# First layer's attention in a transformer kernel: heads handled in pairs that lie on different halves of the partitions, and six score buffers in place of three

## The chip, the core and the metric

The kernel runs on one core of a Trainium2 chip. A core has TensorE (matrix products, results in the eight banks of PSUM), VectorE, ScalarE, GpSimd and SyncE, which issues most transfers; they run side by side and wait for each other through semaphores. The metric is the device time of one execution in microseconds (us), as the median of several runs. Beside it stands one execution that was recorded by the profiler, with the start and duration of every instruction.

## What is computed

Two blocks on 256 tokens of 1024 features, in float32. The first block has an attention layer and a retention layer, each with a SwiGLU product and modulated by adaLN; the second block has two hybrid layers (convolution, latent attention, dilated attention). The change touches the attention of the first layer: 16 heads of 64 features, eight with stick-breaking and eight with a causal softmax (MoBA with one block of 256 keys, which is its own block, so that nothing else is selected).

```python
def stick_breaking_attention(q, k, v):
    ...
        z = jnp.einsum('bhqd,bhkd->bhqk', qb, k).astype(jnp.float32) * scale
        qpos = start + jnp.arange(SB_QBLOCK)
        strict = kpos[None, :] < qpos[:, None]
        log_1mb = jnp.where(strict, jax.nn.log_sigmoid(-z), 0.0)
        after = lax.cumsum(log_1mb, axis=3, reverse=True) - log_1mb
        a = jnp.where(strict, jnp.exp(jax.nn.log_sigmoid(z) + after), 0.0)
        return jnp.einsum('bhqk,bhkd->bhqd', a.astype(v.dtype), v)
...
def moba_attention(q, k, v):
    ...
        s_own = jnp.einsum('bhqd,bhkd->bhqk', qb, k_own).astype(jnp.float32) * scale
        kpos_own = own * MOBA_BLOCK + kpos_in
        s_own = jnp.where(kpos_own[None, :] <= qpos[:, None], s_own, NEG)
        p = jax.nn.softmax(jnp.concatenate([s_past, s_own], axis=-1), axis=-1).astype(v.dtype)
        ...
def attn_hybrid_mixer(h, w_qkv, w_o, pos):
    ...
    sb = stick_breaking_attention(q[:, :N_SB_HEADS], k[:, :N_SB_HEADS], v[:, :N_SB_HEADS])
    qm = rotary(q[:, N_SB_HEADS:], pos)
    km = rotary(k[:, N_SB_HEADS:], pos)
    mb = moba_attention(qm, km, v[:, N_SB_HEADS:])
    o = jnp.concatenate([sb, mb], axis=1).transpose(0, 2, 1, 3).reshape(B, S, ATT_W)
    return o @ w_o
```

## The kernel before

Every large product is done in three parts (mm3, L381): activations and weights are each split into a high and a low part in TensorE's faster float32 form, and hi*hi, hi*lo and lo*hi are summed. The split of the weights is made on the chip: SyncE loads a chunk of 128 x 2048 into one of a few `raw` buffers (L325), ScalarE casts it (whi, L345), VectorE subtracts (wlo, L346). In the same buffers come the weights of adaLN, which VectorE multiplies and sums as a side task (acc, L541); `rate` says how many such steps are added per weight chunk. Their results are split (L456, L457) and broadcast by TensorE with ones_r.

The order on TensorE is written out by hand: it runs its instructions in the order in which the program emits them. A planner keeps a clock `now` of planned TensorE work. A side task is a generator (Job) that yields for how long to leave it alone; `tick`, called behind each mm3, runs the tasks whose due time has come. The other engines' order is set by the compiler's scheduler, which prefers what was emitted earlier and takes what is ready by its own model.

In layer0 (L786) `startup` makes the modulation, the first norm, and q, k (ps0) and v of the stick-breaking heads. Then main products on w_qkv for q, k and v of the MoBA heads run (gemm_col), and the attention of the first eight heads is a side task among them; MoBA's attention is a side task among the product for v and the output product on w_ao (gemm_k). A head of 64 features lies on one half of the 128 partitions of qT and kT: even heads on partitions 0 to 63, odd heads on 64 to 127.

- sb_job (L621) takes one stick-breaking head: two score products into a bank of PSUM (of 256 and of 128 columns, each done as two passes in the trace), three ScalarE steps Abs, Exp, Ln into a tile sbe (three buffers, L629 to L631), two VectorE steps that form the masked sums in a tile named sbs (tag sm, three buffers, L632, L634); after D_SB = 9.42 us of planned work three products with a triangle (ntri) and with minus ones (sq in the trace) on top of the scores, then Exp on ScalarE (L639) and the mask on VectorE (L640) into aT.
- causal_job (L587) takes one MoBA head (and one MLA head in the second block): two score products, masked maximum on VectorE (L598), Exp with sum on ScalarE (L602), reciprocal (L604), normalisation (L606); after D_SOFT = 11.39 us of planned work three transposes (L281) and a copy into aT (L608). The tile sm has three buffers in layer 0.
- score (L830) is the task of one head; it waits till q and k are there. Heads are spawned with due times SP_SB = 2.55 and SP_MB = 2.65 us apart. av (L839) does the products with v of two heads when all eight heads are done; their results lie on different halves of the columns of the array.
- epi (L821) turns a block of q or k of the MoBA heads by the rotary factors on VectorE (L582 to L585, tiles rows and rt) out of the block's bank; D_ROT0 = 5.49 us later they are transposed and copied (L828) to qT, kT.

A bank of PSUM comes from one pool of eight (`bank`). It is free when its last reader is done.

## Time and profile before

| | |
|---|---|
| time, median of 3 runs | 1525.12 us (1524.68 to 1526.28) |
| profiled execution, its span | 1522.7 us |
| TensorE (PE) busy | 1487.4 us, 98% |
| weight loads (PEld) busy | 1237.7 us, 81% |
| VectorE (DVE) busy | 1026.6 us, 67% |
| ScalarE (ACT) busy | 800.0 us, 53% |
| GpSimd (POOL) busy | 93.0 us, 6% |
| DMA, mean | 201 GB/s |

TensorE's products overlap: a product starts before the one ahead of it has ended, so the distance between starts, not the duration, is what a product costs in a stream. Shares of the whole span hide that stages have different limits; the stage of the change lies between 69 and 167 us. PE, PEld, DVE, ACT, POOL and SP are the engines' names in the rows; a q behind a name is the engine's instruction queue. L277 is the line of every matrix product, L281 that of every transpose: they are told apart by the tiles.

### The profile page before, as it was taken

What the parts mean: (1) busy time and instruction counts of PE and PEld (TensorE: products, weight loads), DVE (VectorE), ACT (ScalarE), POOL (GpSimd) and SP (SyncE); (2) the same over time, 40 slices, a digit from 0 to 9 for tenths busy, and PEclk for the clock granted to TensorE, in tenths of its full rate; (3) what the DMA queues carried; (4) which work ended last, traced back from release to release, by engine and by line L of the source; (5) the groups of instructions that cost most, each with busy time, mean ns of one, the idle gap of its engine ahead of it and who ended that gap; (6) DMA issues with size and microseconds to landing.
All of it is one profiled execution on the core that took longest, in us unless ns stands there. A gap on an engine that the chain in (4) does not pass through costs nothing.

```text
span 1522.7 us, 19655 instructions
## 1 busy us (share of the span) xinstructions
PE 1487.4 (98%) x7508; PEld 1237.7 (81%) x7508; DVE 1026.6 (67%) x1605; ACT 800.0 (53%) x1297; POOL 93.0 (6%) x84
## 2 busy tenths in 40 slices
PE   7989999999999999999999999999999999999998
PEld 4776788887877888888787899988888779998887
DVE  4698888748988767655577565555666866555564
ACT  4657455534544544544457655565545765555551
POOL 0000000000010000000020011100001101111000
PEclk9999999999999999999999999999999999999999
DMA  9667587755776648654355354444545535444442
GB/s 381 258 227 273 204 293 296 276 187 193 294 256 241 228 144 301 236 195 173 109 185 182 124 196 157 163 169 170 180 159 184 179 129 192 159 159 176 176 172 81
DMA packets 52961, 306.62 MB, mean 201 GB/s; under 512 B 7546, under 2 KB 10490, under 8 KB 24580
## 3 DMA queue, kind: packets, MB, share of 16 engines
q1 hardware_dynamic: 52148, 305.14, 55.9%
q8 instruction: 59, 0.97, 0.3%
q10 hardware_dynamic: 720, 0.24, 0.1%
q14 instruction: 34, 0.28, 0.1%
HBM read 301.16 MB, written 1.05 MB: 198 GB/s over the span
## 4 chain that ended last, share of the span: by engine, by line
PE 85%; DVE 6%; DMA 3%; ACT 2%; POOL 1%; issue 1%; DVEq 0%; POOLq 0%; ACTq 0%
PE p L277 81%; PE p L281 5%; DMA raw<-in_w_in_dram 3%; DVE wlo L346 2%; ACT whi L345 1%; POOL qss L452 1%; POOL ss L485 1%; DVE junk L493 0%; DVE res L520 0%; DMA raw<-in_w_ao_dram 0%; DVE acc L541 0%; DMA x<-in_x_dram 0%; DVE x L521 0%; ACT sm L602 0%; ACT sbe L630 0%
## 5 line engine op out<-in xcount | busy, mean ns | idle before, releaser
L346 DVE TENSOR_TENSOR wlo<-raw,whi 128x1024 fp32r<-128x1024 f32 (+2 forms) x474 | 541.7, 1162 | 196.4 <-ACT whi L345 191.1
L345 ACT CAST whi<-raw 128x1024 fp32r<-128x1024 f32 (+2 forms) x474 | 467.9, 1002 | 290.2 <-PE p L277 209.9
L277 PE MATMUL p<-whi,hh 128*128 128x512 f32 (+1 forms) x1504 | 590.9, 393 | 6.8 <-ACT mqT L1223 3.8
L277 PE MATMUL p<-whi,hl 128*128 128x512 f32 (+1 forms) x1504 | 566.8, 377 | 3.2 <-DVE hl L457 2.7
L277 PE MATMUL p<-wlo,hh 128*128 128x512 f32 (+1 forms) x1504 | 565.5, 376 | 0.0
L277 PEld LDWEIGHTS p<-whi,hh 128*128 128x128 f32 x1504 | 283.3, 188 | 56.3 <-issue 6.7
L277 PEld LDWEIGHTS p<-whi,hl 128*128 128x128 f32 x1504 | 282.9, 188 | 49.9 <-DVE hl L457 3.9
L277 PEld LDWEIGHTS p<-wlo,hh 128*128 128x128 f32 x1504 | 283.9, 189 | 40.6 <-issue 1.7
L541 DVE SCALAR_TENSOR_TENSOR acc<-raw,csc,acc 128x1024 f32<-128x1024 f32 x80 | 102.4, 1280 | 4.9 <-DMA raw<-in_ada_w_dram 4.0
L277 PE MATMUL p<-whi,ah 128*128 128x512 f32 x176 | 70.0, 398 | 0.0
L277 PE MATMUL p<-whi,al 128*128 128x512 f32 x176 | 69.5, 395 | 0.0
L277 PE MATMUL p<-wlo,ah 128*128 128x512 f32 x176 | 69.5, 395 | 0.0
L452 POOL TENSOR_TENSOR dss<-dss,mh 128x6 f32<-128x6 f32 x32 | 42.3, 1322 | 345.7 <-DVE dss L451 328.7
L1337 DVE TENSOR_TENSOR rows<-p,dss 128x384 f32<-128x384 f32 x32 | 17.9, 558 | 45.6 <-POOL dss L452 45.6
L916 ACT ACTIVATE fth<-p 128x256 f32<-128x256 f32 x44 | 16.9, 383 | 58.1 <-PE p L277 58.0
L485 POOL TENSOR_TENSOR ss<-ss,mh 128x1 f32<-128x1 f32 x14 | 13.8, 988 | 489.9 <-DVE ss L484 489.9
L277 PE MATMUL p<-whi,s 128*128 128x512 f32 x128 | 41.3, 397 | 0.0
L277 PEld LDWEIGHTS p<-whi,al 128*128 128x128 f32 x176 | 33.0, 187 | 8.1
L277 PEld LDWEIGHTS p<-wlo,ah 128*128 128x128 f32 x176 | 33.0, 188 | 7.8
L277 PEld LDWEIGHTS p<-whi,ah 128*128 128x128 f32 x176 | 33.0, 188 | 7.8
L277 PEld LDWEIGHTS p<-dk,dq 64*128 64x128 f32 x256 | 30.8, 187 | 9.8 <-issue 8.0
L277 PE MATMUL p<-whi,yh 128*128 128x512 f32 x96 | 38.4, 400 | 0.0
(251 smaller groups left out, 1579.7 us busy)
## 6 DMA issues: line engine op xcount, KB each, us to landing
raw<-in_w_in_dram SPq DMA_DIRECT2D x48, 1024.0 KB, 4.8
raw<-in_w_gu_dram SPq DMA_DIRECT2D x44, 1024.0 KB, 5.9
raw<-in_ada_w_dram SPq DMA_DIRECT2D x40, 1024.0 KB, 6.8
raw<-in_w_in_dram SPq DMA_DIRECT2D x48, 768.0 KB, 4.5
raw<-in_w_ret_dram SPq DMA_DIRECT2D x24, 1024.0 KB, 5.0
raw<-in_w_dn_dram SPq DMA_DIRECT2D x22, 1024.0 KB, 4.9
raw<-in_w_qkv_dram SPq DMA_DIRECT2D x11, 1024.0 KB, 5.6
as<-in_ada_s_dram SPq DMA_DIRECT2D x16, 512.0 KB, 8.5
```

Source lines behind the costliest of these rows:

```text
L277: self.T.matmul(out, lhsT=lhsT, rhs=rhs, start=first, stop=last, skip_group_check=skip)
L281: self.T.transpose(out, in_, self.ident)
L345: for ins in (self.A.copy(hi[:, :m * n], src), self.V.tensor_tensor(lo[:, :m * n], src, hi[:, :m * n].bitcast(F32), ALU.subtract)):
L346: self.V.tensor_tensor(lo[:, :m * n], src, hi[:, :m * n].bitcast(F32), ALU.subtract)):
L452: self.G.tensor_tensor(ss, ss, self.mh[:, :n], ALU.pow)
L485: self.G.tensor_tensor(ss[:, 0:1], ss[:, 0:1], self.mh[:, 0:1], ALU.pow)
L541: self.V.scalar_tensor_tensor(acc, r[:, j * D:j * D + D], self.sc[:, k:k + 1], acc, ALU.mult, ALU.add)
L916: A.activation(th, ps[:, 0:256], AF.Silu)
L1337: V.tensor_tensor(rows[:, :384].rearrange("p (h d) -> p h d", d=64), ps.rearrange("p (h d) -> p h d", d=64), ss[:, :6, None].to_broadcast( ...
```

## The change

Heads of the first layer are taken in pairs. score now stands for a pair: both heads get their aT tile and their bank at once, and the score products alternate: the first product of the even head (partitions 0 to 63), the first of the odd head (64 to 127), then the second of each. All ScalarE and VectorE steps of the two heads follow, head by head. The second steps (products with ntri and nones, or transposes) come for the first head after the same planned delay, and for the second head D_SB2 = 1.8 (stick-breaking) or SP_MB = 2.65 us (MoBA) later. Stick-breaking pairs are spawned 6.2 us apart, MoBA pairs 2 x 2.65. The planned cost of a pair's score products is that of one head. The tag sm has six buffers in layer 0 in place of three, and the stick-breaking scratch e (three buffers of the same size) is gone: the head's own aT tile holds it. MLA calls the same new function with one head; its planned cost is 0.218 in place of 0.214 for the first product, everything else there is as before.

```diff
-SP_SB, SP_MB, SP_MLA, SP_DIL = 2.55, 2.65, 13.59, 4.5
+SP_SB, D_SB2, SP_MB, SP_MLA, SP_DIL = 6.2, 1.8, 2.65, 13.59, 4.5
...
-    def causal_job(self, q, k, scale, aT):
+    def causal_heads(self, heads, scale, gap):
         V, A = self.V, self.A
-        qT, kT = q(), k()
-        ps = self.bank()
-        self.mm(ps[:, 0:128], qT[:, 0:128], kT[:, 0:128])
-        self.mm(ps[:, 128:384], qT[:, 128:256], kT, us=0.432)
-        sm = self.ph.tile([128, 384], F32, tag="sm", bufs=self.smb, name=self.nm("sm"))
...
+        n = len(heads)
+        ps = [self.bank() for _ in heads]
+        for p, (qT, kT, _) in zip(ps, heads):
+            self.mm(p[:, 0:128], qT[:, 0:128], kT[:, 0:128], us=0.218 / n)
+        for p, (qT, kT, _) in zip(ps, heads):
+            self.mm(p[:, 128:384], qT[:, 128:256], kT, us=0.432 / n)
...
-        yield D_SOFT if self.smb != 2 else D_SOFTM
-        A.copy(aT, self.trs(sm, 3))
+        yield D_SOFT if n == 2 else D_SOFTM
+        for i, (sm, (_, _, aT)) in enumerate(zip(sms, heads)):
+            if i:
+                yield gap
+            A.copy(aT, self.trs(sm, 3))
...
-    def sb_job(self, q, k, aT):
+    def sb_heads(self, heads, gap):
+
         V, A = self.V, self.A
-        qT, kT = q(), k()
-        ps = self.bank()
-        self.mm(ps[:, 0:256], kT[:, 0:128], qT, True, True, 0.432, True)
-        self.mm(ps[:, 256:384], kT[:, 128:256], qT[:, 128:256], False, True, 0.216, True)
-        e = self.ph.tile([128, 384], F32, tag="sbe", bufs=3, name=self.nm("sbe"))
-        sp = self.ph.tile([128, 384], F32, tag="sm", bufs=self.smb, name=self.nm("sbs"))
...
+        ps = [self.bank() for _ in heads]
+        for p, (qT, kT, _) in zip(ps, heads):
+            self.mm(p[:, 0:256], kT[:, 0:128], qT, True, True, 0.216, True)
+        for p, (qT, kT, _) in zip(ps, heads):
+            self.mm(p[:, 256:384], kT[:, 128:256], qT[:, 128:256], False, True, 0.109, True)
...
+        for p, (_, _, aT) in zip(ps, heads):
+            e = aT.rearrange("p j n -> p (j n)")
+            sp = self.ph.tile([128, 384], F32, tag="sm", bufs=self.smb, name=self.nm("sbs"))
+            A.activation(e, p[:, :384], AF.Abs)
...
         yield D_SB
...
+        for i, (p, sp, (_, _, aT)) in enumerate(zip(ps, sps, heads)):
+            if i:
+                yield gap
+            self.mm(p[:, 0:256], self.ntri, sp[:, 0:256], False, True, 0.432, True)
...
-            self.ph, self.smb = p, 3
+            self.ph, self.smb = p, 6
...
-            for hd in range(8):
-                sj[hd] = self.spawn(score(hd, j0), 1.0 + hd * SP_SB)
             for pr in range(4):
...
+                sj[pr] = self.spawn(score(pr, j0), 1.0 + pr * SP_SB)
+            for pr in range(4):
...
-            for hd in range(8, 16):
-                sj[hd] = self.spawn(score(hd, qkj), 0.5 + (hd - 8) * SP_MB)
+            for pr in range(4, 8):
+                sj[pr] = self.spawn(score(pr, qkj), 0.5 + (pr - 4) * 2 * SP_MB)
```

## Rows read from the trace of the kernel before

**Rows 1.** Busy time by stretch: stretch, length, engines, clock, DMA share, GB/s

```profile
82.00:98.00 16.00, 12.62 (x70) 10.84 (x71) 15.56 (x27) 8.82 (x17) 0.00 (x0) 1.00 0.63 224
129.00:146.50 17.50, 15.46 (x72) 10.68 (x70) 16.77 (x42) 15.88 (x47) 0.00 (x0) 1.00 0.69 248
167.00:300.00 133.00, 133.00 (x607) 109.11 (x607) 109.10 (x126) 66.93 (x98) 4.33 (x4) 1.00 0.78 286
```

**Rows 2.** TensorE's timeline, stick-breaking: start us, us, instruction, count

```profile
71.45 2.06 PE L277 MATMUL p<-qT,kT 64*128 64x256 f32 x16 [0.35 <-ACT qT L815]
...
75.41 0.39 PE L277 MATMUL p<-whi,hl 128*128 128x512 f32 x1
...
76.91 0.39 PE L277 MATMUL p<-wlo,hh 128*128 128x512 f32 x1
...
88.13 1.04 PE L277 MATMUL p<-sbs,sq 128*128 128x256 f32 x6
88.92 0.47 PE L277 MATMUL p<-whi,hh 128*128 128x512 f32 x1
```

**Rows 3.** TensorE's timeline, MoBA's first scores

```profile
114.16 1.46 PE L277 MATMUL p<-kT,qT 64*128 64x256 f32 x10 [0.47 <-ACT kT L828]
115.55 0.50 PE L277 MATMUL p<-whi,hh 128*128 128x512 f32 x1
...
116.45 0.92 PE L277 MATMUL p<-kT,qT 64*128 64x128 f32 x4
```

**Rows 4.** TensorE's timeline, products with v and the output product's end

```profile
146.47 2.82 PE L277 MATMUL p<-aT,v 128*64 128x256 f32 x32
...
157.02 0.39 PE L277 MATMUL p<-acch,ones_r 128*128 128x512 f32 x1
...
157.95 0.39 PE L277 MATMUL p<-whi,oTq 128*128 128x512 f32 x1
...
163.56 1.03 PE L281 MATMUL p<-ident,junk 128*128 128x128 f32 x8
```

**Rows 5.** TensorE's timeline, its longest wait in the first layer

```profile
97.78 0.63 PE L281 MATMUL p<-ident,rows 128*128 128x128 f32 x4 [3.38 <-DVE rows L585]
```

**Rows 6.** Waits from 60 to 170 us: who for whom, us, times, longest

```profile
PE p L281 <- DVE rows L585: 3.7, 2, 3.4
...
PE p L277 <- ACT aT L608: 1.0, 2, 0.7
PE p L281 <- ACT sm L606: 0.9, 2, 0.7
...
PEld p L277 <- ACT qT L828: 0.6, 1, 0.6
ACT sm L606 <- DVE st L604: 0.5, 2, 0.3
```

**Rows 7.** VectorE's timeline in the first layer's attention

```profile
74.32 0.56 DVE L632 SCALAR_TENSOR_TENSOR sbs<-p,sbe 128x384 f32<-128x384 f32 x1 [1.22 <-ACT sbe L631]
...
87.71 0.56 DVE L632 SCALAR_TENSOR_TENSOR sbs<-p,sbe 128x384 f32<-128x384 f32 x1 [0.43 <-PE p L277]
...
94.22 1.28 DVE L541 SCALAR_TENSOR_TENSOR acc<-raw,csc,acc 128x1024 f32<-128x1024 f32 x1
95.41 0.42 DVE L584 TENSOR_TENSOR rt<-p,rope 128x256 f32<-128x256 f32 x1
...
103.16 1.23 DVE L346 TENSOR_TENSOR wlo<-raw,whi 128x1024 fp32r<-128x1024 f32 x1 [0.82 <-ACT whi L345]
...
119.44 0.28 DVE L598 CUSTOM_DVE_ANT_0 sm<-p,causal 128x128 f32<-128x128 f32 x1
...
129.02 0.29 DVE L598 CUSTOM_DVE_ANT_0 sm<-p,causal 128x128 f32<-128x128 f32 x1 [1.88 <-PE p L281]
```

**Rows 8.** ScalarE's timeline, the last copy of probabilities

```profile
144.47 0.48 ACT L608 COPY aT<-p 128x384 f32<-128x384 f32 x1
```

**Rows 9.** SyncE's timeline, the load of the last chunk of w_ao

```profile
131.52 0.34 SPq L325 DMA_DIRECT2D raw<-in_w_ao_dram  x1
```

More of the change, by code (lines that the diff above doesn't have):

```diff
@@ new lines, in causal_heads @@
+        n = len(heads)
[4 more added lines that the diff above has]
+            self.mm(p[:, 128:384], qT[:, 128:256], kT, us=0.432 / n)
+        halves = ((0, 128), (128, 384))
+        sms = []
+        for p in ps:
+            sm = self.ph.tile([128, 384], F32, tag="sm", bufs=self.smb, name=self.nm("sm"))
+            st = self.wk.tile([128, 6], F32, tag="st", bufs=8, name=self.nm("st"))
+            for t, (c0, c1) in enumerate(halves):
+                V.tensor_tensor_reduce(sm[:, c0:c1], p[:, c0:c1], self.causal[:, c0:c1], 1.0, NEG, ALU.add, ALU.max,
+                                       st[:, t:t + 1])
+            V.tensor_scalar_mul(st[:, 2:4], st[:, 0:2], -scale)
+            for t, (c0, c1) in enumerate(halves):
+                A.activation(sm[:, c0:c1], sm[:, c0:c1], AF.Exp, bias=st[:, 2 + t:3 + t], scale=scale,
+                             accum_out=st[:, 4 + t:5 + t])
+            V.reciprocal(st[:, 4:6], st[:, 4:6])
+            for t, (c0, c1) in enumerate(halves):
+                A.activation(sm[:, c0:c1], sm[:, c0:c1], AF.Copy, scale=st[:, 4 + t:5 + t])
+            sms.append(sm)
@@ new lines, in sb_heads @@
+        ps = [self.bank() for _ in heads]
[3 more added lines that the diff above has]
+            self.mm(p[:, 256:384], kT[:, 128:256], qT[:, 128:256], False, True, 0.109, True)
+        d2 = lambda x: x.rearrange("p (j n) -> p j n", n=128)[:, 0:3:2]
+        sps = []
+        for p, (_, _, aT) in zip(ps, heads):
+            e = aT.rearrange("p j n -> p (j n)")
+            sp = self.ph.tile([128, 384], F32, tag="sm", bufs=self.smb, name=self.nm("sbs"))
+            A.activation(e, p[:, :384], AF.Abs)
+            A.activation(e, e, AF.Exp, scale=-1.0)
+            A.activation(e, e, AF.Ln, bias=1.0)
+            V.scalar_tensor_tensor(sp, p[:, :384], 0.0, e, ALU.max, ALU.add)
+            V.tensor_tensor(d2(sp), d2(sp), self.strict, ALU.mult)
+            sps.append(sp)
@@ L828, in epi, with score @@
                 A.copy((qT if b == 1 else kT)[1][:, :, t * 128:t * 128 + 128], self.trs(rows, 4))
-            def score(hd, deps):
-                j, r = hd // 8, hd % 8
-                pr, o = r // 2, (r % 2) * 64
+            def score(pr, deps):
+                j, r = pr // 4, pr % 4
                 while not all(d.done for d in deps):
                     yield 0.7
-                aTs[hd] = aT = p.tile([128, 3, 128], F32, tag="aT", bufs=AT0, name=self.nm("aT"))
-                q, k = (lambda: qT[j][o:o + 64, pr]), (lambda: kT[j][o:o + 64, pr])
-                yield from self.sb_job(q, k, aT) if j == 0 else self.causal_job(q, k, 0.125, aT)
+                heads = []
+                for i in range(2):
+                    aTs[2 * pr + i] = aT = p.tile([128, 3, 128], F32, tag="aT", bufs=AT0, name=self.nm("aT"))
+                    heads.append((qT[j][64 * i:64 * i + 64, r], kT[j][64 * i:64 * i + 64, r], aT))
+                yield from self.sb_heads(heads, D_SB2) if j == 0 else self.causal_heads(heads, 0.125, SP_MB)
             def av(pr, deps):
@@ L849, in layer0 @@
             ch = chunks_of(D, QKV_BLOCKS)
-            for hd in range(8):
-                sj[hd] = self.spawn(score(hd, j0), 1.0 + hd * SP_SB)
             for pr in range(4):
-                avj[pr] = self.spawn(av(pr, [sj[i] for i in range(8)]), 1.0)
+                sj[pr] = self.spawn(score(pr, j0), 1.0 + pr * SP_SB)
+            for pr in range(4):
+                avj[pr] = self.spawn(av(pr, [sj[i] for i in range(4)]), 1.0)
             qkj = self.gemm_col(h, "w_qkv", ch[1:3], epi, 1)
-            for hd in range(8, 16):
-                sj[hd] = self.spawn(score(hd, qkj), 0.5 + (hd - 8) * SP_MB)
+            for pr in range(4, 8):
+                sj[pr] = self.spawn(score(pr, qkj), 0.5 + (pr - 4) * 2 * SP_MB)
             vj = self.gemm_col(h, "w_qkv", ch[3:4], epi, 3)
             for pr in range(4, 8):
-                avj[pr] = self.spawn(av(pr, vj + [sj[i] for i in range(8, 16)]), 1.0)
+                avj[pr] = self.spawn(av(pr, vj + [sj[i] for i in range(4, 8)]), 1.0)
             gate, = self.finish(jobs[0])
@@ L1292, in pair @@
                 aTs.append(p.tile([128, 3, 128], F32, tag="maT", bufs=4, name=self.nm("maT")))
-                yield from self.causal_job(lambda: qT[:, hd], lambda: kT[:, hd], 96.0 ** -0.5, aTs[j])
+                yield from self.causal_heads([(qT[:, hd], kT[:, hd], aTs[j])], 96.0 ** -0.5, 0.0)
             yield 1.5
```

25 lines of the change are left out of this document (4 added, 21 removed).

## Prediction, made before the changed kernel ran

> **What bounds the kernel now.** I read the page's first section for the balance of the engines, then the busy time by stretch, then TensorE's timeline through the stretch that the change touches, then the waits and the timelines of VectorE and ScalarE there. The table by stretch says where a saving counts [rows 1]. From 167 us TensorE is busy 133.00 of 133.00 us: what the first layer gains by then is kept, since nothing behind it waits for another engine for long. In the first layer's attention, 69 to 167 us, it is not so: VectorE is busy 15.56 of 16.00 us from 82 to 98, ScalarE 15.88 of 17.50 us from 129 to 146.5. The granted clock is 1.00 in these stretches, so durations of one may be used in another. Three engines take turns as the limit here, and the gain is what the other two leave of TensorE's saving.
>
> **What a head's score product costs on TensorE.** A head alone is four passes, two of 256 and two of 128 columns, on 64 partitions. The last main product (512 columns) before one starts at 75.41, the second one behind it at 76.91: 1.50 us [rows 2], in which two products at their usual distance of 0.23 (four from 157.02 to 157.95, [rows 4]) take 0.46. So a head alone costs 1.04 us. How much of that is streaming? Six passes of the second step (two of 256, four of 128 columns) take from 88.13 to 88.92 [rows 2], so some 0.2 and 0.1 us each, and four score passes some 0.6. The other 0.4 us surrounds them.
>
> Do two halves of the partitions run side by side? The kernel before shows it where heads happen to be neighbours: ten passes (six of 256, four of 128 columns) lie between 114.16 and 115.55, 1.39 us with the surroundings [rows 3], where one after the other they would stream 1.6 and need 2.0. And eight heads' products with v, which alternate between halves of the columns, take 2.82 us for 32 passes [rows 4] that would stream 4.8. I take full overlap: a pair costs what a head alone costs, 1.04. Bounds: 1.04 (full) and 1.6 (0.6 + 0.6 + 0.4, none).
>
> On the surroundings the Trainium skill speaks too: "TensorEngine Tiling (Array Packing)", section "Tiling Modes", says that a change of the tiling mode, not of the tile, drains TensorE. The 0.4 us agrees, and by that page a switch would be paid per pair and not per head, as in the sum here.
>
> **The change part by part.** *Stick-breaking half (heads 0 to 7).* Before, heads 0 to 3 come in one group (71.45, 16 passes) and heads 4 to 7 alone [rows 2]. After, counting the planner's due times along the products of the trace, the first two pairs still come together, since the second's due time has passed when the transposes before it are done; pairs 2 and 3 stand alone. The two lone pairs save 2 x 1.04 = 2.08. In the first group head 0 waits for the second half of kT in any case; alternating may save some 0.4 (0 to 0.7). Together 2.5 us of TensorE.
>
> Does it arrive? At 97.78 TensorE waits 3.38 us for VectorE's rotary rows [rows 5], and once more for 0.3 before MoBA's scores (3.7 in two waits, [rows 6]). Up to there VectorE has three gaps of note: 1.22 (the first head's ScalarE chain), 0.43 (TensorE's head 7) and 0.82 (ScalarE's cast, which waits for TensorE to free a weight buffer) [rows 7]. Its instructions are not changed. The three extra score buffers let sums of heads 3 to 5 be written before the second products of heads 0 to 2 have read theirs: that fills VectorE earlier, it does not shorten its list. So the start of the next half, which waits for the last rotary rows, moves by what these gaps give back. The 0.43 and the 0.82 end with TensorE, so I let them go: 1.25 us; the 1.22 stays. Bounds: 0 and 2.5. What TensorE saves beyond that becomes a longer wait for rotary rows. It may come out better, since the 3.38 arises because accumulations for ada of 1.28 us stand in VectorE's queue between the rotary's steps [rows 7], and an earlier demand may be scheduled ahead of them; that I don't count.
>
> The second product of a pair's second head comes 1.8 us of planned work behind the first's, and the logarithm's scratch moves into the head's own aT tile, with no instruction more or less. Both cost nothing while TensorE has main products to place there, and one step of three, 0.70 us, where not.
>
> *MoBA half (heads 8 to 15).* Before: heads 8 to 10 in a group, 11 to 15 alone (head 11 is shown, the others repeat it four times, [rows 3]). After: 8 to 11 in the group, in the same time, and two lone pairs: 1.04 + 2 x 1.04 = 3.1 us saved on TensorE. Its waits from 114 on are 0.47 for kT [rows 3], 1.0 for aT copies and 0.9 for ScalarE's normalisation [rows 6], 2.4 in all.
>
> What is late next is ScalarE: through its softmax work, up to 144.95, the end of the last copy of probabilities [rows 8], it waits for VectorE only 0.5 us in two places [rows 6]. Those are the chain of the fourth head and the fifth: VectorE idles 1.88 at 129.02 [rows 7] until TensorE's transposes free the first of three score buffers. With six they need not wait. I take half of it, 0.25, since the scheduler sets ScalarE's order anew; bounds 0 and 0.5. So the last copy ends at 144.95 - 1.25 - 0.25 = 143.45.
>
> Behind it must follow the second products of four pairs (2.8), half of the output product (16 steps of 0.70 = 11.2) and two ada pairs (0.93) [rows 4]: 14.9. Before, the output product ends at 163.56 [rows 4], 18.6 behind the last copy, because five more steps of its first half (two before the second products, which start at 146.47, three behind them: 3.5 us) were still to do. TensorE can now do them earlier: it must win 3.5 + 1.5 = 5.0 us by then and has 3.1 (products), up to 2.4 (waits) and 1.25. End: 143.45 + 0.2 + 14.9 = 158.55, a gain of 1.25 + 0.25 + 3.5 = 5.0 us. Bounds of this half alone: 1.0 (the 0.25 and one step) and 5.5 (3.1 + 2.4).
>
> *The rest.* MLA calls the same function with one head: same instructions, same order; its planned cost moves by 0.004 us per product, which can at most move a job by one step (0.70 either way). No transfer is added. But SP's loads wait for VectorE to free raw buffers, so a new order on VectorE moves them. The last chunk of w_ao is issued at 131.52 [rows 9], while its part of the product begins behind 149: 17 us, in which the load, two casts and two differences find place; were that cover used up, each further us would be lost.
>
> Sum against the profiled execution: span 1522.7 less 5.0 = 1517.7. The median of the runs is 1525.12, 2.4 above the span, for what lies around it: 1520.1.
>
> **The rivals.** *VectorE and ScalarE keep their pace.* MoBA's chain starts when VectorE reaches the first masked maximum, 119.44, some 4 us behind the scores, since accumulations stand ahead of it [rows 3, 7]; TensorE's saving then becomes waits in front of 143, and only 1 to 2 us pass. For it: TensorE's waits from 97 to 142 end with VectorE or ScalarE [rows 5, 6]. Against it: the 3.5 us of product behind ScalarE's last copy are TensorE's own. Time: 1522.7 - 1.5 + 2.4 = 1523.6. Chance 0.25.
>
> *The ninth bank.* A pair takes two of the eight PSUM banks at once. Before, about 81, six heads, a main product and a transpose fill all eight; head 6 waits 0.6 us for ScalarE to empty one [rows 6]. After, pair 2 stands at about 73.0 + 8 x 0.70 + 1.04 = 79.6, with four older heads, the finished main product's bank and the transposes' bank; the next main product needs a ninth. If the transposes' copy comes at once, TensorE loses some 0.9. If that bank is instead given by VectorE's rotary, which in the order of before ends its reading at 95.83 [rows 7], TensorE stands for up to 15 us. It then has 6 steps (4.2), 7 second products (0.8 each, 5.6) and a pair (1.04) more to do than before had at 97.78. So up to 97.78 - 10.8 = 87.0 this only takes the old wait's place; beyond it each us counts against the 5.0 - 1.25 = 3.75 of the MoBA half, and from 87.0 + 3.75 + 3.0 = 93.8 the kernel is measurably slower. At 95.83 it loses 8.8 - 3.75 = 5.1: 1530.2. Against it: in the order of due times the rotary stands ahead of later work, and ScalarE has room. Chance 0.09.
>
> The same page of the Trainium skill, section "Gotcha 1: PSUM Pressure", warns that row tiling raises the pressure on PSUM; the 0.6 us wait for a bank agrees with it.
>
> *The halves do not overlap.* Then a pair costs 1.6 instead of 2.08, TensorE saves 4 x 0.48 + 0.3 = 2.2, and some 1 to 2 pass: 1523.6. Against it stand [rows 3, 4]. Chance 0.04.
>
> **How the numbers follow.** The forecast, the chain through ScalarE with five steps moved ahead of its end: 0.62, 1520.1, own range 1517 to 1522. For 8 in 10 the range has to reach into the first rival. Low end: 5.5 in the MoBA half and 2.5 in the other, 8.0 us: 1517.1; with 0.7 for a moved step, 1516.4. High end: the first rival's 1523.6 with 0.9 lost at a bank, 1524.5. A measurement of this kernel can tell about 0.2%, 3.0 us, from no change, so faster means below 1522.1. Of the forecast 0.60 lies there and 0.02 above; of the two rivals without much gain 0.28 lie within and 0.01 below; the bank is slower, 0.09. Faster 0.61, same 0.30, slower 0.09.
>
> **What would show it.** A pair alone takes about 0.9 us for its eight passes; if 1.5, the halves do not overlap. The masked maximum of head 11 no longer stands behind a transpose. MoBA's scores start near 112. ScalarE's last probability copy ends near 143.5, the second products directly behind it, with no first-half steps of the output product behind them, and the output product ends near 158.6. From there on every stage lies 5 us earlier with the same busy time. Wrong would be: waits for rotary rows or for a bank between 79 and 100 that sum to more than 3.4 + 2.5, or ScalarE's last copy at 145 or later.

## The result, and the profile after

The changed kernel takes 1536.55 us (median; 1535.63 to 1538.93), and the kernel before takes 1524.90 beside it: a ratio of 1.0067 with a 95% interval of 1.0048 to 1.0086. The forecast was 1520.1, a gain. The profiled execution has a span of 1535.4 us against 1522.7, which is 12.7 more.

The overlap itself is there. TensorE's timeline of the changed kernel (start us, length us, instruction, count, in brackets the wait before it and who ended it):

```profile
74.36 1.62 PE L277 MATMUL p<-qT,kT 64*128 64x256 f32 x16 [0.35 <-ACT qT L832]
...
81.59 0.92 PE L277 MATMUL p<-qT,kT 64*128 64x256 f32 x8
82.44 0.65 PE L281 MATMUL p<-ident,rows 128*128 128x128 f32 x4
85.59 0.79 PE L277 MATMUL p<-whi,hh 128*128 128x512 f32 x1 [2.49 <-ACT qT L845]
86.18 0.63 PE L277 MATMUL p<-wlo,hh 128*128 128x512 f32 x1
86.61 0.63 PE L277 MATMUL p<-whi,hl 128*128 128x512 f32 x1
...
118.62 0.63 PE L281 MATMUL p<-ident,rows 128*128 128x128 f32 x4 [4.40 <-DVE rows L585]
119.18 3.25 PE L277 MATMUL p<-kT,qT 64*128 64x128 f32 x16
122.36 2.01 PE L277 MATMUL p<-aT,v 128*64 128x256 f32 x19
...
126.30 0.93 PE L277 MATMUL p<-kT,qT 64*128 64x128 f32 x8
...
161.42 0.50 PE L277 MATMUL p<-acch,ones_r 128*128 128x512 f32 x1 [0.79 <-ACT acch L456]
164.28 0.79 PE L277 MATMUL p<-accl,ones_r 128*128 128x512 f32 x1 [2.36 <-DVE accl L457]
...
177.18 1.94 PE L281 MATMUL p<-ident,junk 128*128 128x128 f32 x8 [2.90 <-DVE junk L495]
```

Four heads' first scores take 1.62 us where [rows 2] has 2.06, and a lone pair's eight passes take 0.92. But waits of 2.49, 4.40, 0.79, 2.36 and 2.90 us stand in these rows (and two of 1.4 between 127 and 145 us outside them), where before had one of 3.38 [rows 5] and no other above 0.8. The products behind the first of these waits follow each other by 0.43 us and no longer by 0.23, and the products of the stick-breaking heads with v (`aT,v` at 122.36) now come behind MoBA's first scores; before they ran from 107.22, ahead of them. The feed-forward norm's first transposes, at 163.56 in [rows 4], are at 177.18.

Busy time by stretch of the changed kernel (stretch, length, then TensorE, its weight loads, VectorE, ScalarE, GpSimd, granted clock, DMA share, GB/s); the first three answer to [rows 1], the others are four stretches inside at half the clock, 1.2 of 2.4 GHz:

```profile
82.00:98.00 16.00, 13.51 (x68) 10.89 (x65) 15.01 (x20) 8.62 (x19) 0.00 (x0) 0.79 0.77 286
129.00:146.50 17.50, 16.05 (x85) 12.52 (x84) 11.47 (x31) 16.21 (x42) 0.95 (x1) 1.00 0.18 61
167.00:300.00 133.00, 129.58 (x581) 105.48 (x580) 106.56 (x129) 64.54 (x99) 4.83 (x4) 0.97 0.72 264
...
85.00:91.80 6.80, 6.21 (x15) 4.87 (x16) 6.80 (x11) 2.53 (x4) 0.00 (x0) 0.50 0.95 330
119.10:122.50 3.40, 3.40 (x20) 2.25 (x20) 3.37 (x12) 1.02 (x4) 0.00 (x0) 0.50 1.02 366
163.50:170.30 6.80, 6.02 (x14) 4.76 (x15) 5.49 (x7) 0.88 (x3) 0.95 (x1) 0.50 0.80 281
177.20:180.60 3.40, 2.96 (x10) 2.02 (x10) 3.40 (x7) 2.03 (x5) 0.00 (x0) 0.51 0.45 188
```

In 129 to 146.5 the transfers fall from 248 to 61 GB/s and VectorE from 16.77 to 11.47 us, while ScalarE stays full. SyncE's timeline says why, first before, then after:

```profile
117.85 3.44 SPq L325 DMA_DIRECT2D raw<-in_ada_w_dram  x2
125.50 0.24 SPq L533 DMA_DIRECT2D acc<-in_ada_b_dram  x1
131.52 0.34 SPq L325 DMA_DIRECT2D raw<-in_w_ao_dram  x1
134.76 3.34 SPq L325 DMA_DIRECT2D raw<-in_ada_w_dram  x2
```

```profile
117.90 3.65 SPq L325 DMA_DIRECT2D raw<-in_ada_w_dram  x2
136.79 0.33 SPq L325 DMA_DIRECT2D raw<-in_w_ao_dram  x1
138.94 0.25 SPq L533 DMA_DIRECT2D acc<-in_ada_b_dram  x1
146.01 1.46 SPq L325 DMA_DIRECT2D raw<-in_ada_w_dram  x2
```

The last chunk of w_ao is now issued ahead of the third modulation's bias. It waits 15.2 us for a raw buffer, until VectorE's subtraction wlo, behind ScalarE's cast of the same weights, has freed one. ScalarE (after) reaches those casts, and the split of the second modulation's sums, only behind softmax work:

```profile
132.33 0.51 ACT L607 ACTIVATE sm<-sm,st 128x256 f32<-128x256 f32 x1
132.73 0.20 ACT L607 ACTIVATION_READ_ACCUMULATOR sm<-sm,st 128x1 f32 x1
132.82 1.04 ACT L345 CAST whi<-raw 128x1024 fp32r<-128x1024 f32 x1
133.76 0.81 ACT L611 ACTIVATE sm<-sm,st 128x128 f32<-128x128 f32 x2
134.46 1.05 ACT L345 CAST whi<-raw 128x1024 fp32r<-128x1024 f32 x1
135.40 1.05 ACT L456 CAST acch<-acc 128x1024 fp32r<-128x1024 f32 x1
...
150.53 0.48 ACT L617 COPY aT<-p 128x384 f32<-128x384 f32 x1 [3.35 <-PE p L281]
```

Before, that split is at 122.13. So the third modulation's sums are ready (`accl`) at 164.2 us instead of 148.2, and its product blocks TensorE's queue ahead of the rest of the output product.

The chain that ended last, from the start of MoBA's scores to the norm, its shares by line, first before (113 to 170 us), then after (113 to 182):

```profile
by line: PE p L277 55.8%; ACT sm L602 6.2%; ACT sm L606 5.3%; DVE res L520 4.5%; ACT whi L345 4.5%; DVE x L521 4.2%; ACT aT L608 2.6%; DVE junk L493 2.5%; DVE junk L495 2.1%; DVE bc L557 2.1%; DVE sm L598 2.0%; DVE wlo L346 1.5%; issue 1.4%
```

```profile
by line: PE p L277 17.3%; DMA raw<-in_w_gu_dram 12.7%; ACT sm L607 10.3%; DVE wlo L346 9.1%; DVE acc L541 8.9%; ACT sm L611 8.2%; ACT whi L345 5.6%; issue 3.4%; DVE accl L457 3.3%; DVE x L521 2.7%; DVE res L520 2.6%; POOL ss L485 2.1%; DVE 
```

Before, TensorE carried this stage; after, softmax, casts, sums and loads do.

**The account of the stage.** For each kernel's profile I take S, the start of the first stick-breaking scores (71.45 before, 74.36 after), and F, the first feed-forward product (165.34 and 178.94). The time S to F is split into stretches in which no product ran (idle), half of the busy time at clock 0.50 (clock), and the rest (work). "Sums ready" is the end of the last modulation's accl, and "sums to F" the time from there to F. Before and the run with the buffers alone, below, have the same products in the same order and differ by 1.3 in "work", so it is good to about that.

| kernel (label) | ratio to before, 95% | S to F | work | idle | clock | sums ready, from S | sums to F |
|---|---|---|---|---|---|---|---|
| before | 1 | 93.9 | 86.8 | 7.1 | 0.0 | 76.8 | 17.1 |
| after | 1.0048 to 1.0086 | 104.6 | 79.6 | 16.3 | 8.7 | 89.9 | 14.7 |
| bufs | 0.9989 to 1.0016 | 96.1 | 85.5 | 7.9 | 2.7 | 81.9 | 14.2 |
| sb_pairs | 1.0045 to 1.0078 | 105.0 | 81.7 | 17.6 | 5.7 | 94.9 | 10.0 |
| mb_pairs | 1.0003 to 1.0032 | 97.4 | 83.9 | 10.6 | 2.9 | 85.5 | 12.0 |
| after3 | 1.0048 to 1.0079 | 102.9 | 81.0 | 14.3 | 7.6 | 81.1 | 21.8 |
| fill_after2 | 1.0058 to 1.0088 | 102.6 | 92.8 (11 of it fillers) | 9.7 | 0.0 | 91.1 | 11.5 |
| pair2_later | 1.0016 to 1.0035 | 98.3 | 81.6 | 12.7 | 4.0 | 88.3 | 10.0 |
| av_early | 0.9993 to 1.0020 | 94.9 | 81.6 | 11.0 | 2.2 | 82.9 | 12.0 |
| after_rot | 1.0037 to 1.0082 | 100.2 | 81.4 | 13.2 | 5.6 | 88.0 | 12.2 |
| before_rot | 1.0038 to 1.0073 | 103.1 | 85.5 | 13.9 | 3.7 | 93.4 | 9.7 |
| pairs_late_q | 0.9986 to 1.0016 | 92.8 | 81.5 | 9.6 | 1.7 | 80.9 | 12.0 |
| before_late_q | 0.9980 to 1.0010 | 94.1 | 86.3 | 6.1 | 1.7 | 80.6 | 13.5 |
| fill_after | 1.0096 to 1.0136 | 109.1 | 103.5 (23 of it fillers) | 5.5 | 0.0 | 92.7 | 16.3 |
| fill_before | 0.9984 to 1.0004 | 96.5 | 92.8 (6 of it fillers) | 3.7 | 0.0 | 80.1 | 16.5 |
| best | 1.0001 to 1.0035 | 97.5 | 80.9 | 13.4 | 3.2 | 85.7 | 11.8 |
| after_cut | 1.0040 to 1.0086 | 100.2 | 79.6 | 15.3 | 5.2 | not waited for | |
| fill_cut | 1.0020 to 1.0045 | 104.4 | 86.3 (6 of it fillers) | 13.9 | 4.2 | not waited for | |
| after_rl2_3 | 1.0016 to 1.0048 | 96.8 | 81.0 | 11.1 | 4.7 | 69.6 | 27.2 |
| av_rl2_3 | 1.0041 to 1.0083 | 103.1 | 80.6 | 13.7 | 8.9 | 81.1 | 22.1 |

So 12.7 = 2.9 ahead of S + 10.7 in the stage - 0.9 behind F, and 10.7 = -7.2 work + 9.2 idle + 8.7 clock. The saved work is there; waits and clock took two and a half times as much. The 2.9 ahead of S isn't the change's: the five engines run the same instructions in the same order there, and the clock was low for 10.2 us in this execution and 6.8 in that of before (by profile 6.8 to 13.7 us; before_late_q, single heads, has 10.2 and S at 74.26).

The same stretch from S to F by engines, in the columns of the table by stretch, for before, after and pairs_late_q:

```profile
71.45:165.34 93.89, 86.77 (x453) 65.61 (x453) 83.33 (x150) 62.42 (x136) 3.44 (x4) 1.00 0.62 227
74.36:178.94 104.58, 88.30 (x452) 68.19 (x453) 86.57 (x152) 61.91 (x135) 4.32 (x4) 0.91 0.59 214
73.96:166.78 92.82, 83.25 (x452) 63.73 (x453) 83.72 (x150) 62.08 (x136) 3.40 (x4) 0.98 0.62 230
```

VectorE's list does not get shorter with the pairs: it is busy 83 to 87 us here in every run but fill_after (88.9), and what differs is its idle time, 10.6 us before, 18.0 after, 9.1 in pairs_late_q.

### The profile page after: what moved, and what is told of

Same layout as the page of the kernel before. It is cut to its first block, busy times and chain, and to the rows that moved or that the text cites. A ratio compares the mean times of both kernels' runs of the same rounds, so it can differ in the third digit from the quotient of the medians.

```text
span 1535.4 us, 19646 instructions
## 1 busy us (share of the span) xinstructions
PE 1493.5 (97%) x7508; PEld 1243.4 (81%) x7508; DVE 1026.9 (67%) x1605; ACT 800.1 (52%) x1297; POOL 93.6 (6%) x84
## 4 chain that ended last, share of the span: by engine, by line
PE 83%; DVE 7%; DMA 4%; ACT 3%; POOL 1%; issue 1%; SPq 0%; POOLq 0%; ACTq 0%; DVEq 0%
PE p L277 78%; PE p L281 5%; DVE wlo L346 3%; DMA raw<-in_w_in_dram 2%; ACT whi L345 1%; DMA raw<-in_w_ao_dram 1%; DMA raw<-in_w_gu_dram 1%; POOL qss L452 1%; DVE acc L541 1%; ACT sm L607 0%; POOL dss L452 0%; DVE junk L493 0%; ACT sm L611 0%; POOL ss L485 0%; DMA x<-in_x_dram 0%
## 5 line engine op out<-in xcount | busy, mean ns | idle before, releaser
L277 PE MATMUL p<-dk,dq 64*128 64x128 f32 x256 | 36.9, 284 | 1.8 <-DVE dk L1362 1.8
```

What stands on the lines that cost most here:

```text
L277: self.T.matmul(out, lhsT=lhsT, rhs=rhs, start=first, stop=last, skip_group_check=skip)
```

## Experiments

**Which part of the change loses?** The runs are the buffers alone, each half alone, and the pairs with three buffers. The first expectation defines the theories 1 to 3 that the others use; SB stands for stick-breaking.

```diff
 bufs:     single heads, self.smb = 6, e = aT.rearrange("p j n -> p (j n)")
 sb_pairs: bufs, and sb_heads for heads 0 to 7 (SP_SB 6.2, D_SB2 1.8)
 mb_pairs: bufs, and causal_heads in pairs for heads 8 to 15
 after3:   the changed kernel with self.smb = 3
```

> The kernel before with six score buffers instead of three and the exponentials of a SB head written into its aT tile; heads still one at a time. Theory 1 (TensorE's waits of the SB half, above all the 2.49 us at 83 us for a bank, and the granted clock of 0.79 behind them in 82 to 98) and theory 2 (in the MoBA half the weights' buffers come free late, SyncE's raw tiles stand at 117.9 to 136.8, the last accumulation of ada comes at 158.8 instead of 145.9) both put the loss on the pairs: this kernel within 2 us of 1524.9. Theory 3 (six buffers let the score steps of six heads run ahead of the weights' casts on ScalarE and VectorE): 1529 to 1534, with the last accumulation of ada behind 150 us.

It took 1526.23 us against 1526.82, no difference. The buffers alone are not the cause.

> SB heads in pairs as in the changed kernel, MoBA heads one at a time as before; six score buffers. Theory 1: the whole loss starts here, 1530 to 1537, with a TensorE wait of 2 to 3 us near 83 us and a granted clock of about 0.8 in 82 to 98. Theory 2: at most the 3.1 us that the changed kernel lost between its first SB scores (74.36) and its first MoBA scores (119.18 against 113.20 before), 1522 to 1528. Theory 3: as in the run with the buffers alone.

It took 1535.88 us, the whole loss. The wait of 2.49 near 82 is there, but the stretch 82 to 98 has clock 1.00, so theory 1's sign for the clock failed; what grew most is the wait for the last modulation's sums:

```profile
166.89 0.80 PE L277 MATMUL p<-acch,ones_r 128*128 128x512 f32 x1 [7.42 <-ACT acch L456]
```

> MoBA heads in pairs as in the changed kernel, SB heads one at a time as before; six score buffers. Theory 1: the SB half is that of before, so 1519 to 1525, and the saving of the overlap shows (eight passes of a pair in about 0.93 us). Theory 2: the MoBA half loses by itself, 1529 to 1534, with SyncE's raw tiles of w_ao held until behind 130 us and the last accumulation of ada behind 150 us. Theory 3: as in the run with the buffers alone.

It took 1530.71 us, 3.9 more than before at the medians (0.03 to 0.32%). That lies in theory 2's range, and its sign is there (the last accumulation starts at 154.6 us), though the loss is a third of the whole. Its work falls, its idle and clock rise by more. The two halves lose 9 and 4 alone and 10 to 12 together, so the losses aren't sums of parts.

> The changed kernel with three score buffers, as before, instead of six. Theory 1 and theory 2: the order on TensorE is that of the changed kernel and the softmax steps of the third pair wait for a buffer, so no gain against the changed kernel's 1536.5: 1534 to 1542. Theory 3: the loss goes with the buffers, 1522 to 1529.

It took 1535.89 us, as the changed kernel. Theory 3 is out. The order was not quite that of the changed kernel: MoBA's scores come at S + 38.7 (after: 44.8) without the wait of 4.40, and the time is the same, so that wait alone is not the loss either.

**Is it the clock?** Over 52 executions of these kernels the span follows the mean granted clock (correlation -0.90): 0.993 before, 0.988 after, about what 8 us at full clock would make. A low stretch begins in or just behind a wait of TensorE: at 84.99 in the wait that ends at 85.59, at 119.12 behind the one that ends at 118.62. Fillers, products that nobody reads, keep TensorE at work in the waits:

```diff
     def trs(self, rows, m, w=128, fill=0):
         pt = self.bank()
+        for _ in range(fill):
+            self.T.matmul(pt[:, 0:128], lhsT=self.ident, rhs=self.ident, start=True, stop=True, ...)
```

> The changed kernel with products of the unit matrix, whose results nobody reads, put into four stretches in which TensorE stood: 16 ahead of the transposes of q's first token tile (the wait of 2.49 us at 83.1), 36 ahead of those of k's second (4.40 at 114.2), 28 ahead of the last modulation product (0.79 and 2.36 at 160.6) and 24 ahead of the first transposes of the feed-forward norm (2.90 at 174.3). They fit into the waits, so nothing real is later. Theory 1 (the waits themselves cost only a part; behind each of them the granted clock is half for 3.4 to 6.8 us): the four low stretches between 85 and 181 us go, 20.5 us at half clock or 10.2 us: 1526 to 1531, mean clock 0.993 or more. Rival (the clock falls for another reason, and the time is the waits' own): 1535 to 1540, mean clock 0.988.

It took 1543.93 us, slower by 7 still. My sizes were wrong: a filler is two records, 0.11 us apart, so the 104 took some 23 us. What it does show: no low clock from 21.6 to 185.4 us.

> The run with the filled waits again, with the fillers cut to the waits. One filler takes TensorE 0.21 us (two records of 0.107), twice what the first trial counted, so its 104 took 22 us where 12.9 us of waits were there; now 8, 18, 13 and 11, 10.7 us in all. Theory 1: the clock stays at 1.00 from 27 to 181 us as in the first trial, and nothing real is later: 1526 to 1531, mean clock 0.993. Rival (the waits' own length is all): 1535 to 1538.

It took 1535.18 us, with the clock at 1.00 from 27.7 us to the end of the work and a mean of 0.995, and no gain: theory 1 falls. Of 15.3 us of idle and clock gone, 11 are fillers (50 of 0.22 us) and 2.2 other work; only 2.0 reach F. The sums are ready at S + 91.1 as before the fillers (89.9), and F follows 11.5 behind. So the correlation is not the price of the clock here: another engine is late, TensorE waits, and the clock falls into time that TensorE had to spare. The Trainium skill, "TensorE: Matmul & The Clock Gate", section "Terms", prices time at half clock at half of it. As an estimate by that page, the fillers should have given back the 8.7 us; the measured 2.0 decides.

> The kernel before with 28 such products ahead of the transposes of q's second token tile, where TensorE stood 3.38 us at 94.4. In the profile of before the clock did not fall there, in that of the run with the buffers alone it fell from 96.6 to 103.4 us behind the same wait. Theory 1: where it falls it costs 3.4 us, so the median comes down by 1 to 3 us, to 1523.5 to 1526, and the mean clock rises from 0.993 to 0.995. Rival: no change, 1526.8.

It took 1526.14 us against 1526.26 (0.9984 to 1.0004), with the same over-sized fillers (28, some 6 us into 3.38), and a mean clock of 0.994 to 0.996 against 0.993. It can't price the clock: F came 2.6 later from S.

**Is it the order?** Two constants of the planner change where things stand.

```diff
 pair2_later: SP_SB 6.2 -> 6.6
 av_early:    SP_SB 6.2 -> 5.1, and sb_heads yields 6.5 instead of D_SB (9.42)
```

> The changed kernel with SP_SB 6.6 instead of 6.2: the planner now starts q's second product, with its bank, ahead of the third pair's scores. Everything behind is planned as in the changed kernel (the SB half's output products behind the first MoBA scores). If the ninth bank is the main cause: the 2.49 us wait at 83.1 and the low clock of 85.0 to 91.8 go, 1529 to 1532. If the order behind (output products after the MoBA scores, accumulations of ada late) is: 1534 to 1538, with a wait of about 4 us ahead of the MoBA scores as now.

It took 1529.76 us: some 7 us won by 0.4 in one constant, and the number expected if the ninth bank is the main cause. The wait for a ninth bank is gone, but MoBA's scores come at S + 37.0 (after: 44.8) too, so the bank isn't alone in it. The products with v still stand behind MoBA's scores, and the sums are still late, with waits of 4.98 and 1.28 for them.

> The changed kernel with SP_SB 5.1 (two of the old steps of 2.55) instead of 6.2 and a planned delay of 6.5 instead of 9.42 us from a SB pair's scores to its second products. The SB half's output products stand again ahead of k's last transposes, as in the kernel before, instead of behind the first MoBA scores; the third pair's scores come earlier still, so the wait for the ninth bank is not removed. If the order behind is the main cause: the wait of 4.4 us before the MoBA scores falls under 1.5 us, MoBA scores start near 113 us and not 119.2, SyncE's raw tiles come free as before and the last modulation product has no wait: 1524 to 1529. If the ninth bank is: 1533 to 1538.

It took 1526.85 us, level with before. My reading that the bank wait would stay was wrong: two pairs' second products now stand between the transposes and the product that needs the bank, and fill the time of ScalarE's activations. One long wait is left, for q's second rotary:

```profile
82.17 0.60 PE L281 MATMUL p<-ident,rows 128*128 128x128 f32 x4
82.60 1.92 PE L277 MATMUL p<-sbs,sq 128*128 128x256 f32 x12
84.70 0.50 PE L277 MATMUL p<-whi,hh 128*128 128x512 f32 x1 [0.18 <-ACT qT L845]
...
96.84 1.09 PE L281 MATMUL p<-ident,rows 128*128 128x128 f32 x4 [5.42 <-DVE rows L585]
```

> The changed kernel with the four steps of each rotary put ahead of the accumulations of ada and the casts on VectorE (first() around the call). If the accumulations between the rotary's steps make the wait of 4.40 us ahead of the MoBA scores: that wait falls under 1.5 us and the low clock of 119.1 to 122.5 us with it; the wait for the ninth bank at 83 stays, and the accumulations come later still, so that the last modulation product may wait longer: 1529 to 1534. If VectorE's order has no part in it: 1535 to 1538.

```diff
+                with self.first():
                     self.rotary(rows, ps, rope, t, 8, 32)
```

It took 1532.10 us: the 4.40 wait is gone (MoBA's scores at S + 35.6), and the waits for the sums are 4.04 and 2.16. The wait for the ninth bank, expected to stay, is gone as well:

```profile
82.54 0.47 PE L277 MATMUL p<-whi,hh 128*128 128x512 f32 x1 [0.29 <-DVE rt L584]
```

So a kernel without either wait, whose MoBA scores start 6 us earlier from S than before, still loses by 0.37 to 0.82%: the two waits ahead of MoBA's scores don't set the time by themselves. From MoBA's scores to F it takes 64.6 us, against 59.8 after and 52.1 before. The same edit on the two others:

> The run with the output products early (SP_SB 5.1, delay 6.5) with each rotary first on VectorE as well. Its profile had one long wait left before 130 us, 5.42 us at 91.4 for q's second rotary, and behind it half the clock from 94.5 to 101.3 us. If both go: 5.4 of wait and 3.4 of clock less what other steps then wait for, 1519 to 1524, the first version under the kernel before. If the wait passes on to another step (the accumulations behind the rotary): 1525 to 1529.

It took 1528.87 us against 1525.5 (1.0001 to 1.0035): the wait of 5.42 is gone, and two of 4.11 and 3.71 are new. The wait passed on.

> The kernel before with each rotary first on VectorE: what the order of VectorE alone is worth without pairs. If its wait of 3.38 us at 94.4 us goes and with it the low clock that follows it in most runs: 1521 to 1525. If the wait passes on: 1525 to 1529. The difference between this and the run of the pairs with the same order is what the pairs are worth: 3 to 5 us if TensorE's saved passes arrive, none if VectorE or ScalarE keep the pace.

It took 1532.58 us with single heads and no pairs at all, above both ranges. VectorE's order alone makes a loss of this size (1.0038 to 1.0073), with a wait for the sums:

```profile
163.74 0.80 PE L277 MATMUL p<-acch,ones_r 128*128 128x512 f32 x1 [9.69 <-ACT acch L456]
```

**Do the sums set the time?** These runs take the wait for them away, or bring their loads forward.

```diff
 after_cut, fill_cut (with fillers 8 and 18 at 83.1 and 114.2):
+        if (l, v) == (0, 4):
+            hi, lo = self.prev_hl
 after_rl2_3, av_rl2_3: R_L0 2.04 -> 2.3 in the changed kernel, in av_early
```

> The changed kernel, in which the product of layer 0's last modulation (the gain ahead of the feed-forward norm) reads the split sums of the modulation before it instead of its own; its own loads and accumulations still run, but nobody waits for them. Left out: that modulation's own value. Theory 2 (the modulations' chain on SyncE, VectorE and ScalarE comes 16 us later than before, and the last product stands in TensorE's queue ahead of the rest of the output product): the waits of 0.79 and 2.36 us at 160.6 to 164.3 go, and what follows the sums, 10 to 12 us to the first feed-forward product in most runs so far, no longer sets it: 1527 to 1531, with the first feed-forward product at 169 to 173 us instead of 178.9. Rival (the waits and the clock ahead of 145 us set the time, the chain has slack as before): 1534 to 1537.

It took 1534.92 us: no measurable gain, where 1527 to 1531 was expected. The waits for the sums are gone and the output product ends 93.2 us behind S instead of 99.9, but then the norm is late and takes most of it back; F is 4.4 earlier from S, and behind F this execution is 6.3 us longer, 4.9 of it clock:

```profile
169.85 1.94 PE L281 MATMUL p<-ident,junk 128*128 128x128 f32 x8 [5.20 <-DVE junk L495]
```

VectorE reads the gain's product there behind the second tile's residual; before, ahead of it.

> The same cut, and the waits at 83.1 and 114.2 us filled with 8 and 18 idle products as in the second trial of fillers, so that the clock stays. That trial showed the clock at 1.00 and no gain. If that was so because the last modulation's sums (ready at 166.0 us) set the time then, the clock is worth its price once they don't: 3 to 5 us under the run with the cut alone, 1523 to 1527. If the clock is worth nothing anyhow: equal to the run with the cut.

It took 1531.03 us, 3.9 less than the cut alone, which is the 3 to 5 expected if the clock counts once the sums don't (though not the 1523 to 1527). But its profile has F at S + 104.4, no better, so I don't call this shown.

> The changed kernel with R_L0 2.3 instead of 2.04 (modulation steps fed per weight chunk), so the loads of the third modulation's bias and first chunks are issued ahead of the fourth chunk of w_ao, as in the kernel before, and the planner puts the SB half's output products ahead of k's last transposes again. Theory 2: the last sums are ready before 153 us instead of 164.2, no TensorE wait for them; the wait for the ninth bank at 83 stays: 1523 to 1530. Rival (the ninth bank and the clock behind it): 1532 to 1537.

It took 1530.38 us. The sums are ready at S + 69.6, 20 us earlier than after, no wait for them is left, and half of the loss comes back (1.0032 for 1.0067). Waits of 2.49, 2.94 and 1.51 us are left: the sums are not the whole. The edit also put the products with v ahead of MoBA's scores, so the half isn't the sums' alone.

> The run with the early output products (SP_SB 5.1, delay 6.5), with R_L0 2.3. Its sums were ready at 156.8 us and its first feed-forward product came 12.0 us later, as in most runs. Theory 2: sums before 150 us and the first feed-forward product at 163 to 166 us: 1519 to 1524, under the kernel before. If VectorE then pays with later rotaries (its wait of 5.42 us at 91.4 grows): 1525 to 1529.

It took 1534.90 us, 8 slower than without the earlier loads. The sums are ready at S + 81.1 all the same, and waits of 5.44, 2.37 and 3.24 stand in it. Both ranges are missed on the slow side. Its sums, and those of after3, come as early from S as in pairs_late_q below (80.9), and F comes 10 us later: the time of the sums alone doesn't set F.

**What are the pairs worth in an order that suits them?** In two last runs q's second transposes are moved to where their rows are ready, with pairs and with single heads.

```diff
-                yield D_ROT0
+                yield 9.5 if (b, t) == (1, 1) else D_ROT0      # pairs_late_q: av_early; before_late_q: before, with 8.0
```

> The run with the early output products (SP_SB 5.1, delay 6.5), with the transposes of q's second token tile alone planned 9.5 us behind its rotary instead of 5.49; the order of the loads and of everything else stays. Some 3.5 us of other products then stand ahead of these transposes, where TensorE waited 5.42 us and lost another 2.2 us to the clock. If the pairs' saved passes are worth what TensorE waits less: 1526.8 less 3 to 5, so 1521 to 1524, the first version under the kernel before. If the wait passes on to the modulations' sums (ready at 156.8 us, first feed-forward product 12.0 us later in that run): 1525 to 1528.

It took 1526.17 us against 1526.04 (0.9986 to 1.0016): no gain, the range of a wait that passes on. The wait for q's rows is gone, and one of the same kind stands near it, for VectorE's next masked sums:

```profile
97.09 1.45 PE L277 MATMUL p<-sbs,sq 128*128 128x256 f32 x6 [3.38 <-DVE sbs L647]
```

> The same for the kernel before, with single heads: q's second transposes planned 8.0 us behind the rotary, some 2 to 3 us of other products ahead of them, where TensorE waited 3.38 us. If a wait taken from TensorE counts there: 1526 less 2 to 3, 1523 to 1524.5. If it passes on: no change. The difference between the two runs is what the pairs are worth once TensorE's order suits them: about 5 us by the saved work, 0 if the other engines keep the pace.

It took 1525.65 us (0.9980 to 1.0010), no change. The paired kernel does 4.8 us less work in the stage than the single one (81.5, 86.3), and waits 3.5 more; F comes 1.3 earlier from S, which the medians don't show. The sums are ready at the same S + 80.9 and 80.6. The chain that ended last from 103 to 170 us, first in before_late_q, then in pairs_late_q:

```profile
by line: PE p L277 66.1%; PE p L281 4.3%; ACT sm L602 4.2%; DVE res L520 3.9%; DVE x L521 3.6%; ACT sm L606 3.1%; issue 2.9%; DVE wlo L346 2.9%; DVE junk L493 2.1%; DVE junk L495 1.8%; DVE sm L598 1.4%; DVE bc L557 1.0%; DVE hl L457 0.9%; A
```

```profile
by line: DVE wlo L346 18.3%; DVE acc L541 13.3%; ACT sm L607 9.0%; DMA raw<-in_w_gu_dram 8.6%; ACT sm L611 8.4%; ACT whi L345 5.8%; PE p L277 4.5%; DVE res L520 3.8%; issue 3.8%; DVE x L521 2.9%; DVE junk L493 2.1%; DVE oTk L457 1.9%; PE p 
```

TensorE's products are 66.1% of it with single heads and 4.5% with pairs (47.5% in the kernel before, same stretch). With the order mended, VectorE and ScalarE keep the pace. No version here beats the kernel before.

## Why the prediction was wrong, step by step

- *A pair costs what a head alone costs*: right. 0.92 and 0.93 for eight passes; the first group saves 0.44, where 0.4 was taken. The work saved, 5.6 predicted, is 4.8 between the two late_q kernels and 5 to 7 against before. The rival without overlap is out.
- *Each queue keeps its order*: the step that failed, and it was never written as one. I used the planner's due times only for the first scores, moved everything else by what TensorE saved, wrote of the gap of 1.8 that it would "cost nothing while TensorE has main products to place there, and one step of three, 0.70 us, where not", and gave the pairs' spacing no term at all. The diff has SP_SB 6.2 for two heads, where two old steps are 5.1. With the delay, that puts the last second products and so the products with v behind MoBA's scores, and moves the last loads. av_early, with pairs and six buffers as in the change, changes these two constants alone (to 5.1 and 6.5) and gets 10 us back (1.0067 to 1.0006 of before). Which consequence of the order costs the time is not shown: av_early also hides the bank's wait (0.18 for 2.49), and in pair2_later and after_rot the products with v stay behind while MoBA's scores start 8 to 9 us earlier from S.
- *MoBA's scores start near 112*: 119.18. Of the 6.0 against before, 2.9 come from ahead of S; within the stage S to the scores grew from 41.8 to 44.8 with 3.1 less work: waits of 2.49 and 4.40 and 3.1 of clock. Of the two signs of failure that the prediction named, waits above 3.4 + 2.5 between 79 and 100 didn't come (2.49; the 4.40 stood at 114), ScalarE's last copy behind 145 did.
- *The ninth bank*: the mechanism came, at 0.09. Its place was right (80 to 85 us). The price of 0.9 held "if the transposes' copy comes at once"; it didn't, because the copy stood in ScalarE's queue behind six activations of the pair that held the banks, not behind the rotary, and the wait was 2.49:

```profile
82.55 0.87 ACT L643 ACTIVATE aT<-p 128x384 f32<-128x384 f32 x2 [0.36 <-PE p L277]
83.30 0.94 ACT L644 ACTIVATE aT<-aT 128x384 f32<-128x384 f32 x2
84.13 0.93 ACT L645 ACTIVATE aT<-aT 128x384 f32<-128x384 f32 x2
84.96 0.58 ACT L845 COPY qT<-p 128x512 f32<-128x512 f32 x1
```

  The Trainium skill, "TensorEngine Tiling (Array Packing)", section "Gotcha 1: PSUM Pressure", says that row tiling raises the pressure on PSUM; the trace agrees, with these 2.49 us. Without the wait, in pair2_later, 7 us come back; in after_rot, also without it, 4 at the medians and 1 by the ratios (1.0060 for 1.0067). So the bank alone isn't priced.
- *ScalarE's last copy at 143.45*: 151.0. From MoBA's first scores to that copy it is 31.8 us in both kernels, and 31.7 in bufs, so the 0.25 for six buffers is not there with single heads. With pairs and three buffers (after3) it is 40.0, at the same total time.
- *The output product's end, "two ada pairs (0.93)"*: the mis-built term. I counted these products as TensorE's time and not as a wait for sums that come over SyncE, VectorE and ScalarE. Before, they had slack (F came 17.1 behind them). In seven of the twelve slower runs that wait for them F follows them by 10 to 12 us; in the other five, the changed kernel among them, by 14.7 to 27.2. In the changed kernel they come 13.1 us later from S. That they set the time of the changed kernel alone is not shown: after_cut took the wait away and the norm waited instead; after_rl2_3 brought them 20 us forward, with another order on TensorE, and got half of the loss back.
- *The last chunk of w_ao has 17 us of cover*: its issue moved from 131.52 to 136.79 [rows 9], and what stood behind it in SyncE's queue, the bias and two chunks of the modulation, came 11 to 13 us later with it. I had looked at the load and not at the queue behind it.
- *The granted clock is 1.00*: it wasn't, for 20.5 us from S to just behind F, which made TensorE's work up to F 8.7 us longer. In fill_after2, which kept the clock up, 2.0 of it reached F and nothing the median.
- *VectorE and ScalarE keep their pace*, given 0.25: this is what remains when the order is mended. Its number, 1523.6, is the nearest to pairs_late_q and before (1526.2 and 1526.0 beside each other). In the best order tried, the forecast's 5 us did not arrive either.

What stays open: why the planner's and the scheduler's choices fall as they do for 0.4 us in one constant; which of av_early's two constants does it, since neither ran alone at its value; what the ninth bank and the late sums cost each by itself; and whether the clock is worth something once neither binds.

## What to carry to other kernels

Before a faster step is credited in a kernel whose order comes from a planner, replay that planner for everything queued behind the step (loads, casts, products that wait for another engine's results), and compare the orders of all queues; a constant that paces two items at once must be held against two of the old steps. Look at the chain's shares in the stage itself: where TensorE is 56% of it and the others are nearly full, a saving there is soon theirs. And test a correlation with the clock by keeping the clock up: it can be the shadow of another engine's lateness.

## What the runs showed of the hardware

From S to just behind the first feed-forward product the granted clock fell to 0.50 (1.2 of 2.4 GHz) in waits of TensorE or at most 1.5 us behind them. Most of these waits were of 1.5 to 9.7 us; in after_rot, at 117.7 us, there were only short ones (0.55 and 0.67). It did not fall behind each: the wait of 3.4 to 3.6 us at 94.4 left it at 1.00 in the profile of before and took it down from 96.6 to 103.4 us in that of bufs, with the same products, and the bank's wait of 2.49 us took it down in after and left it at 1.00 in sb_pairs.

Up to S the same instructions took 71.4 to 74.9 us, and the low clock near the start lasted 6.8 us in the shortest and 13.7 in the longest. That agrees with the Trainium skill, "TensorE: Matmul & The Clock Gate", section "Part 1: The HAM clock gate", by which the number of slow products at the start varies between runs of one kernel.

A product of the unit matrix with itself (128 columns, f32) takes TensorE 0.22 us, in two records.
